# Hybrid layer on one core: the last q and k kept in SBUF, state-space gates fetched ahead and turned later, GLU banks swapped, residual loads on GpSimd's queue and later

## The chip, the cores and the metric

The kernel runs on one core of a Trainium2 chip. A core has five engines that run their own instruction streams in order and wait for each other on semaphores: PE (matmuls and transposes), DVE (elementwise), ACT (elementwise with functions), POOL (GpSimd; here it only issues DMAs) and SP (here it only issues DMAs). SBUF is the on-chip memory, PSUM holds what PE writes, HBM is the memory that DMAs reach. The metric is the time of one execution in microseconds (us); lower is better.

## The reference

One layer over 256 positions and 4096 channels, in float32:

```python
h = rmsnorm(x, ln_g)
p_x, p_gate, q, k, v, a_gate, s_u, s_gate = split(h @ w_in)     # 4096 -> 12288 columns
y_pool = pool_mixer(p_x, w_pool, pool_scale)                    # 1024 channels
y_attn = stick_breaking_attention(q, k, v)                      # 16 heads of 128
y_ssm  = s5_mixer(s_u, ...)       # scan, then GELU, then GLU: val * sigmoid(gate), 1024 channels
y = concat(rmsnorm(y_pool) * silu(p_gate), rmsnorm(y_attn) * silu(a_gate),
           rmsnorm(y_ssm) * silu(s_gate))
out = rmsnorm(x + y @ w_out, final_g)
```

In the attention, with z the scaled product of a query and a key, the weight is the exponential of log sigmoid(z) plus the sum, over the keys between, of log(1 - sigmoid(z)). The kernel forms that sum by matmuls with constant triangles (tneg, oneneg).

## The kernel before

**Units.** The work on PE is a row of units, each one block of output columns over all 4096 inputs: 16 narrow input units (512 columns: state-space input, pooling, gates, and v, q, k of the first attention groups), then the wide units w0 (v of groups 2 and 3) and w1 (q and k of group 3; 1024 columns each), then four narrow GLU units (glu0 to glu3, over 1024 inputs), w2 and w3 (gates of the attention), and out0 to out3 (the output projection). A wide unit has 32 sub-blocks of 12 matmuls; steps numbered in SEVEN take two sub-blocks as one seven-product (Strassen) form.

**Weights.** Each sub-block needs 512 KB of weights from HBM. SP's queue loads them into tiles w in the order of the program; LOAD_AHEAD gives four tiles ahead of PE, and two more are lent: tiles of tag u4 in w2 and w3, parts of the big output tile o in the out units. ACT copies a weight tile to its rounded part hi, DVE subtracts it to get lo, and three matmuls make one float32 product: lines 273 to 275 (hi and lo of weights against hi and lo of the rows, xhl, or hhl in the GLU), line 239 for the seven-product form, whose weight differences t DVE makes first.

**Side work.** Attention, state space and gates are written as generators, which `pump` advances between sub-blocks. A tile scheduler then orders the instructions of every engine but SP, whose order is the program's. Tiles come from pools by tag: k4 has six buffers, t4 three, u4 two. PSUM has four double banks in the wide stage: the running unit accumulates in two, and "side" work (products p7, transposes, ps_z, ps_av) uses the other two.

**Attention.** There are four groups of four heads, each in two pairs. For a pair PE makes ps_z from kt and qt and adds a mask (maskb); ACT and DVE make log terms al, split into ah and ax; PE adds the suffix sums of ah and then ax with tneg and oneneg (lines 704 to 706); ACT takes the exponential aw; PE multiplies by vt into ps_av; DVE copies to ao. v, q and k of group 2 and of group 3 go through HBM: `away` and `channels_away` write them (kept_v, kept_q, kept_k), `attention` fetches them, all on GpSimd's queue. Group 2's attention starts at the end of w0, group 3's at the end of w1, so that group 3 runs beside the GLU.

**State-space gates.** The output of the GLU (gl) is normalised by its sums, multiplied by a gate sgb, which GpSimd's queue fetches from HBM, and transposed (line 340) into the rows of the output projection.

**Out units.** At out0's sub-block 10 the big tile o is opened (`start_end`); its space is free after `place` has split the last rows into xhl on DVE (line 98). The residual x is loaded into o (line 892) on SP's queue, in order with the weights. `rows_again` fetches half of one block of rows again (yk, line 382).

Of the kernel before, what the change touches and what calls it, by code (L numbers as in the profile page):

```python
# [68 lines left out]
def body(tc, a, out, ctx):  # L69
# [84 lines left out]
    def load(i):  # L154
        ui, s, h = subs[i]
        kind, c, _ = units[ui]
        lent = i % (LOAD_AHEAD + 2) - LOAD_AHEAD
        if lent >= 0 and state["o"] is not None and kind == "out" and c < 3:
            w = state["o"][:, lent, 3 * WIDE:].rearrange("p (k n) -> p k n", k=2)
        elif lent >= 0 and hhl is not None and kind in WIDE_KINDS:  # L160
            w = mp.tile([P, 2, NU], F32, tag="u4", bufs=2, name="w")
        else:
            w = wp.tile([P, 2, NU], F32, tag="w", bufs=LOAD_AHEAD, name="w")
        nc.sync.dma_start(w, a["ws"][i])
        wtiles[i] = w
# [213 lines left out]

    def rows_again(s):  # L380
        t = bp.tile([P, 2, L], F32, tag="t4", bufs=T4, name="yk")
        nc.sync.dma_start(t, kept[s // 2][:, s % 2 * 2:s % 2 * 2 + 2, :])
        row_sums(s, t[:, 0, :], t[:, 1, :])
        row_difference(t[:, 0, :])
        hi_lo(xhl[:, 2 * s, 0, P:L], xhl[:, 2 * s, 1, P:L], t[:, 0, P:L])
# [277 lines left out]
    aout = {}  # L663
    att_sums = cp.tile([P, 2, 4], F32, name="att_sums")

    def attention(g, vt=None, qt=None, kt=None):
        if vt is None:
            vt, qt, kt = (mp.tile([P, 4, L], F32, tag="k4", bufs=K4, name=k + "t") for k in ("v", "q", "k"))
            for t, k in ((qt, "q"), (kt, "k"), (vt, "v")):
                G.dma_start(t, far[k, g])  # L670
            vt = vt.rearrange("p (t c) m -> p t (c m)", t=2)
            yield
        ao = mp.tile([P, 2, NU], F32, tag="k4", bufs=K4, name="ao")

        for pair in range(2):
            while state["po"] is not None and state["room"] < 7 and not state["draining"]:
                yield
            if state["po"] is None:
                z = pk.tile([P, 4, L], F32, tag="pz", bufs=1, name="ps_z")
            else:  # L680
                z = wide_bank(state["side"], "ps_z").rearrange("p h (c m) -> p (h c) m", c=2)
            state["held"] = True
            z0, z1 = z[:, 0:2, :], z[:, 2, :].rearrange("p (c m) -> p c m", c=2)
            for j in range(2):
                h = 2 * pair + j
                T.matmul(z0[:, j, :], kt[:, h, 0:P], qt[:, h, :], start=j == 0, stop=False, skip_group_check=True)  # L686
                T.matmul(z1[:, j, :], kt[:, h, P:L], qt[:, h, P:L], start=j == 0, stop=False, skip_group_check=True)
            mb = maskb.unsqueeze(1).broadcast_to([P, 2, P])
            T.matmul(z0[:, :, 0:P], identb, mb, start=False, stop=False, skip_group_check=True)
            T.matmul(z1, identb, mb, start=False, stop=False, skip_group_check=True)  # L690
            yield
            zz = z[:, 0:3, :]
            l = apool.tile([P, 3, L], F32, tag="al", bufs=1, name="al")
            log1pexp_parts(zz, l)
            yield
            stt(l, zz, 0.0, l, ALU.max, ALU.add)
            hi = apool.tile([P, 3, L], F32R, tag="ah", bufs=1, name="ah")
            lo = apool.tile([P, 3, L], F32R, tag="ax", bufs=1, name="ax")
            act(hi, l, AF.Copy)
            tt(lo, l, hi.bitcast(F32), ALU.subtract)  # L700
            yield
            for part in (hi, lo):
                l1 = part[:, 2, :].rearrange("p (c m) -> p c m", c=2)
                T.matmul(z0, tneg, part[:, 0:2, :], start=False, stop=False, skip_group_check=True)
                T.matmul(z0[:, :, P:L], oneneg, l1, start=False, stop=part is lo, skip_group_check=True)
                T.matmul(z1, tneg, l1, start=False, stop=part is lo, skip_group_check=True)
            yield
            w = apool.tile([P, 3, L], F32, tag="al", bufs=1, name="aw")
            act(w, zz, AF.Exp)
            yield  # L710
            if state["po"] is None:
                po = pk.tile([P, 2, 2, P], F32, tag="ps", bufs=2, name="ps_av")
            else:
                po = wide_bank(state["side"] + 1, "ps_av")[:, 0, :].rearrange("p (t c m) -> p t c m", t=2, c=2)
            for j in range(2):
                hs = slice((2 * pair + j) * P, (2 * pair + j) * P + P)
                w1 = w[:, 2, j * P:j * P + P]
                T.matmul(po[:, 0, j, :], w[:, j, 0:P], vt[:, 0, hs], start=j == 0, stop=True, skip_group_check=True)
                T.matmul(po[:, 1, j, :], w[:, j, P:L], vt[:, 0, hs], start=False, stop=False, skip_group_check=True)
                T.matmul(po[:, 1, j, :], w1, vt[:, 1, hs], start=False, stop=True, skip_group_check=True)  # L720
            yield
            V.tensor_copy(ao[:, :, pair * L:pair * L + L], po.rearrange("p t c m -> p t (c m)"))
            state["held"] = False
            yield
        square_sums(att_sums, ao, g)
        aout[g] = dp.tile([P, 2, NU], F32, name="kept_a%d" % g)
        G.dma_start(aout[g], ao)
        yield
# [160 lines left out]
    def load_rest(n):  # L889
        o = state["o"][:, :, n * WIDE:n * WIDE + WIDE]  # L890
        for h in range(2):
            nc.sync.dma_start(o[:, :, h * NU:h * NU + NU], a["xr"][2 * n + h])
        return o

    def load_fg(n):
# [4 lines left out]
    def finish(kind, c, n, ps):  # L900
# [34 lines left out]
        elif kind == "glu":  # L935
# [5 lines left out]
            if n % 2 == 0:  # L941
                def gate_gen(y=y):
                    sg = bp.tile([P, 2, NU], F32, tag="t4", bufs=T4, name="gs")
                    glu["sg"] = sg
                    sigmoid_of(y, sg)
                    yield
                side_q.append(gate_gen())
            else:
                def val_gen(y=y, n=n):
                    tt(y, y, glu.pop("sg"), ALU.mult)  # L950
                    yield
                    square_sums(glu_sums, y, n // 2)
                    yield
                    glu[n // 2] = y
                    if n == 3:
                        r = branch_norm(glu_sums, 1024)
                        for u in range(2):
                            yu = glu.pop(u)
                            sg = mp.tile([P, 2, NU], F32, tag="k4", bufs=K4, name="sgb")
                            G.dma_start(sg, sgate[u])  # L960
                            gated(yu, r, sg)
                            yield
                            yield from transposed(yu, keep(2 + u))
                side_q.append(val_gen())
        elif kind in WIDE_KINDS:
            e = state["joined"]
            parts = [(k, scaled_wide(ps, e, h, k + "z")) for h, (k, _) in enumerate(WIDE_IN[c])]
            for h, (k, z) in enumerate(parts):
                if k == "v":
                    away("v", 2 + h, z.rearrange("p t (c m) -> p (t c) m", m=L))  # L970
                elif k in ("q", "k"):
                    side_q.append(channels_away(k, 3, z))
                else:
                    gates.append(att_gate(2 * (c - 2) + h, z))
            if c < 2:
                side_q.append(attention(2 + c))
        elif kind == "out":
            o, e, fg = state["o_n"], state["joined"], state["fg"]
            for t in range(2):
# [10 lines left out]

    gates = []

    def gate_step(at):
        if at in (-1, 0):
            for g in gates:
                next(g)
        elif at in (5, 7):
            for _ in gates[0]:
# [6 lines left out]
    for i, (ui, s, h) in enumerate(subs):  # L1005
# [11 lines left out]
        if s == 0 and h == 0:  # L1017
# [12 lines left out]
            if wide:  # L1030
                ps = start_bank(kind, c)
            elif kind == "glu":
                state["side"] = 2
                pair = wide_bank(c % 2, "pm")
                ps = [pair[:, t, :] for t in range(2)]
            else:
                ps = [pm.tile([P, NU], F32, tag="c%d" % t, bufs=2, name="pm") for t in range(2)]
        if kind == "out" and (c > 0 and at == 0 or c == 0 and at == 10):
            if c == 0:
                start_end()  # L1040
            state["o_n"] = load_rest(c)
        while loaded < min(len(subs), i + 1 + LOAD_AHEAD + (2 if state["o"] is not None or kind in WIDE_KINDS and hhl is not None else 0)):
            if loaded == 0:
                load_first()
            else:
# [32 lines left out]
        if s == nk // 2 - 1 and h == (1 if wide else 0):  # L1078
            n = nth.get(kind, 0)
            nth[kind] = n + 1  # L1080
            if (kind, n) != ("out", 3):
                finish(kind, c if kind in WIDE_KINDS else n, n, ps)
            if gates:
                gate_step(-1)
        if kind == "out" and c == 0 and at == 11:
            rows_again(SEVEN[0])
# [5 lines left out]
                while state["held"]:  # L1092
                    pump(side_q, 1)
        elif wide and gates and at < 31:
            gate_step(at)
        elif wide and 1 <= at < 2 * SEVEN[0]:
            state["room"] = 2 * (2 * SEVEN[0] - at)
            pump(side_q, 2)
# [139 lines left out]
```

## Time and profile before

| | us |
|---|---|
| Three runs | 1558.12, 1563.12, 1563.67 |
| Median | 1563.12 |
| The profiled execution | 1561.29 |
| Its span in the trace | 1559.5 |
| PE busy | 1516.8 (97%) |
| DVE busy | 1268.5 (81%) |
| ACT busy | 899.0 (58%) |
| POOL busy | 16.4 (1%) |
| Mean granted clock of PE | 0.986 |

The span is what the trace covers; 1.8 us of the profiled execution lie around it. Times inside the program are counted from the span's start. The granted clock is the share of full speed that the chip's throttle gave PE. Busy time of an engine is time in which an instruction of it ran, at whatever clock.

### The profile page before, as it was taken

Reading aid. Unit: us, or ns where it says so; the run is one execution under the profiler, and the core shown is the slowest. Engines: PE = TensorE matmul, PEld = TensorE weight load, DVE = VectorE, ACT = ScalarE, POOL = GpSimd, SP = SyncE. Lnnn points to the kernel's source line nnn. Section 1 sums busy time; section 2 is a strip of 40 time slices with the busy share of each in tenths; the row PEclk is TensorE's granted clock in tenths of the full one; section 3 lists DMA queues with packets and bytes.
Section 4 is the critical chain, followed back from the end, with each engine's and each line's share of the span. In section 5 each row is a group of like instructions: output and inputs, shape, how many; then the busy total and the mean of one; then the engine's idle time right before and its main releaser. Section 6 shows DMA issues by size and latency. Waiting matters only on the chain.

```text
span 1559.5 us, 19518 instructions
## 1 busy us (share of the span) xinstructions
PE 1516.8 (97%) x6827; PEld 1232.6 (79%) x6827; DVE 1268.5 (81%) x1933; ACT 899.0 (58%) x1194; POOL 16.4 (1%) x34
## 2 busy tenths in 40 slices
PE   9999999999999999999999999879999799999996
PEld 7888788888787888788888888667888678888885
DVE  7479878898988978897788796558899698888886
ACT  7654546666555655465656556545767464645554
POOL 0000000000000000000000000000000000000000
PEclk9999999999999999999999999889999899999998
DMA  9866556666655656655757466637586476665654
GB/s 359 308 216 201 195 179 201 199 222 202 213 192 189 196 173 194 195 175 187 246 189 249 165 235 200 222 144 240 186 286 218 156 253 220 216 220 199 229 192 172
DMA packets 100978, 328.79 MB, mean 211 GB/s; under 512 B 12432, under 2 KB 18320, under 8 KB 100880
## 3 DMA queue, kind: packets, MB, share of 16 engines
q1 hardware_dynamic: 86416, 300.90, 56.9%
q0 software_dynamic: 4320, 15.73, 2.8%
q10 hardware_dynamic: 10144, 10.92, 2.4%
q8 instruction: 53, 0.87, 0.2%
q14 instruction: 45, 0.37, 0.1%
HBM read 310.73 MB, written 13.63 MB: 208 GB/s over the span
## 4 chain that ended last, share of the span: by engine, by line
PE 90%; DMA 3%; DVE 3%; ACT 2%; issue 1%; SPq 0%; DVEq 0%; ACTq 0%
PE pm L274 24%; PE pm L273 24%; PE pm L275 24%; PE p L239 7%; PE pm L239 5%; DMA w<-in_ws 3%; DVE lo L98 1%; DVE t L98 1%; PE ps_y L649 1%; ACT hi L110 1%; PE ps_z L686 1%; PE ps_c L778 1%; PE ps_bu L622 0%; PE ps_t L340 0%; PE ps_p L431 0%
## 5 line engine op out<-in xcount | busy, mean ns | idle before, releaser
L110 ACT ACTIVATE hi<-w 128x1024 fp32r<-128x1024 f32 (+1 forms) x505 | 509.8, 1017 | 423.3 <-PE pm L275 347.2
L98 DVE TENSOR_TENSOR lo<-w,hi 128x1024 fp32r<-128x1024 f32 (+1 forms) x505 | 587.0, 1170 | 184.6 <-ACT hi L110 182.0
L274 PE MATMUL pm<-lo,xhl 128*128 128x512 f32 x1672 | 655.4, 392 | 0.5 <-DVE lo L98 0.4
L275 PE MATMUL pm<-hi,xhl 128*128 128x512 f32 x1672 | 653.8, 391 | 0.0
L273 PE MATMUL pm<-hi,xhl 128*128 128x512 f32 x1672 | 646.6, 392 | 2.1 <-DVE ss_out L1123 0.8
L273 PEld LDWEIGHTS pm<-hi,xhl 128*128 128x128 f32 x1672 | 314.2, 188 | 72.4 <-issue 2.9
L274 PEld LDWEIGHTS pm<-lo,xhl 128*128 128x128 f32 x1672 | 314.2, 188 | 70.6 <-DVE lo L98 3.0
L275 PEld LDWEIGHTS pm<-hi,xhl 128*128 128x128 f32 x1672 | 314.2, 188 | 67.5 <-issue 2.1
L110 ACT ACTIVATE hi<-t 128x1024 fp32r<-128x1024 f32 x94 | 98.7, 1058 | 63.9 <-DVE t L98 31.8
L98 DVE TENSOR_TENSOR lo<-t,hi 128x1024 fp32r<-128x1024 f32 x94 | 113.2, 1220 | 8.7 <-ACT hi L110 8.2
L239 PE MATMUL p<-hi,xhl 128*128 128x512 f32 x188 | 74.4, 397 | 9.3 <-ACT hi L110 9.1
L239 PE MATMUL pm<-hi,xhl 128*128 128x512 f32 x188 | 75.6, 402 | 2.8 <-ACT hi L110 2.8
L98 DVE TENSOR_TENSOR t<-w 128x512 f32<-128x512 f32 x84 | 54.3, 687 | 29.1 <-DMA w<-in_ws 28.9
L239 PE MATMUL p<-hi,y 128*128 128x512 f32 x188 | 74.0, 394 | 0.1
L98 DVE TENSOR_TENSOR t<-w,t 128x512 f32<-128x512 f32 x84 | 57.5, 685 | 1.5 <-PE ps_t L340 1.2
L107 DVE SCALAR_TENSOR_TENSOR et<-et,pw,tr 128x16 f32<-128x16 f32 (+3 forms) x256 | 55.4, 275 | 2.0 <-ACT tr L110 1.6
L110 ACT ACTIVATE tr<-et,pw 128x32 f32<-128x32 f32 (+3 forms) x128 | 44.2, 382 | 11.1 <-DVE et L107 6.8
L239 PEld LDWEIGHTS p<-hi,xhl 128*128 128x128 f32 x188 | 35.5, 189 | 18.2 <-ACT hi L110 9.6
L239 PEld LDWEIGHTS pm<-hi,xhl 128*128 128x128 f32 x188 | 35.9, 191 | 11.9 <-ACT hi L110 4.1
L239 PEld LDWEIGHTS p<-hi,y 128*128 128x128 f32 x188 | 35.3, 188 | 8.9 <-ACT hi L110 1.0
L637 DVE TENSOR_TENSOR_SCAN tb<-rho,ta 128x256 f32<-128x256 f32 x64 | 40.5, 674 | 0.3
L110 ACT ACTIVATE hi<-o 128x1024 fp32r<-128x1024 f32 (+1 forms) x26 | 25.0, 976 | 24.6 <-PE pm L275 23.6
(266 smaller groups left out, 1286.8 us busy)
## 6 DMA issues: line engine op xcount, KB each, us to landing
w<-in_ws SPq DMA_DIRECT2D x501, 512.0 KB, 4.2
o<-in_ws SPq DMA_DIRECT2D x26, 512.0 KB, 4.3
xsq<-in_xr SPq DMA_DIRECT2D x8, 512.0 KB, 6.7
o<-in_xr SPq DMA_DIRECT2D x8, 512.0 KB, 7.0
xt<-in_xT SPq DMA_DIRECT2D x15, 256.0 KB, 6.1
b<-in_bst ACTq DMA_DIRECT2D x16, 192.0 KB, 4.6
u<-uT ACTq DMA_DIRECT2D x96, 32.0 KB, 2.8
kept<-yT POOLq DMA_DIRECT2D x6, 512.0 KB, 5.6
```

Source lines behind the costliest of these rows:

```text
L98: V.tensor_tensor(o, x, y, op)
L107: V.scalar_tensor_tensor(o, x, s, y, op0, op1)
L110: return S.activation(o, x, f, **kw)
L239: T.matmul(o, stat[:, p, :], pair[q][:, n], start=start and k == 0, stop=stop and k == 2, skip_group_check=True)
L273: T.matmul(ps[t], stat[:, slot, 0, sl], hi[:, n], start=begin, stop=False, skip_group_check=True)
L274: T.matmul(ps[t], stat[:, slot, 0, sl], lo[:, n], start=False, stop=False, skip_group_check=True)
L275: T.matmul(ps[t], stat[:, slot, 1, sl], hi[:, n], start=False, stop=end, skip_group_check=True)
L637: V.tensor_tensor_scan(tb[:, c, :], rho[:, pr:pr + 1].broadcast_to([P, L]), ta[:, c, :], 0.0, ALU.mult, ALU.add)
L649: T.matmul(ps[32 * j:32 * j + 32, 0:L], cf[:, j, c, :], ss[j][:, c, :], start=c == 0, stop=c == 1, skip_group_check=True)
L686: T.matmul(z0[:, j, :], kt[:, h, 0:P], qt[:, h, :], start=j == 0, stop=False, skip_group_check=True)
L778: T.transpose(ps[:, (c * 2 + t) * P:(c * 2 + t + 1) * P], z[:, t, (h * 2 + c) * P:(h * 2 + c + 1) * P], ident)
```

## The change

It has five parts.

1. Attention takes vt, qt and kt from its caller. A function `fetch` loads group 2's v, q and k in one go at the end of w0. Of group 3 only v is fetched, at the end of w1; its q and k are transposed into two SBUF tiles of tag u4 and stay there, ahead of the rest of the side queue. The lent weight tiles of tag u4 are therefore left to w3's sub-blocks alone: w2 has four weight tiles.
2. The state-space gates sgb are fetched when glu3 is written, the product goes into them, and their transposes become steps of w2, at its sub-blocks 5 and 7.
3. The GLU accumulates in banks 2 and 3, its side work uses 0 and 1; before, the other way round.
4. The residual loads and the fetch in `rows_again` go from SP's queue to GpSimd's.
5. The tile o is opened, and its first residual load issued, at out0's sub-block 14 instead of 10.

```diff
@@ load()
-        elif lent >= 0 and hhl is not None and kind in WIDE_KINDS:
+        elif lent >= 0 and kind == "w3":
             w = mp.tile([P, 2, NU], F32, tag="u4", bufs=2, name="w")
@@ rows_again()
-        nc.sync.dma_start(t, kept[s // 2][:, s % 2 * 2:s % 2 * 2 + 2, :])
+        G.dma_start(t, kept[s // 2][:, s % 2 * 2:s % 2 * 2 + 2, :])
@@
-    def attention(g, vt=None, qt=None, kt=None):
-        if vt is None:
-            vt, qt, kt = (mp.tile([P, 4, L], F32, tag="k4", bufs=K4, name=k + "t") for k in ("v", "q", "k"))
-            for t, k in ((qt, "q"), (kt, "k"), (vt, "v")):
-                G.dma_start(t, far[k, g])
-            vt = vt.rearrange("p (t c) m -> p t (c m)", t=2)
-            yield
+    def fetch(g, kinds):
+        got = []
+        for k in kinds:
+            t = mp.tile([P, 4, L], F32, tag="k4", bufs=K4, name=k + "t")
+            G.dma_start(t, far[k, g])
+            got.append(t.rearrange("p (t c) m -> p t (c m)", t=2) if k == "v" else t)
+        return got
+
+    def attention(g, vt, qt, kt):
@@ load_rest()
-            nc.sync.dma_start(o[:, :, h * NU:h * NU + NU], a["xr"][2 * n + h])
+            G.dma_start(o[:, :, h * NU:h * NU + NU], a["xr"][2 * n + h])
@@ finish(), kind "glu"
                         for u in range(2):
-                            yu = glu.pop(u)
-                            sg = mp.tile([P, 2, NU], F32, tag="k4", bufs=K4, name="sgb")
-                            G.dma_start(sg, sgate[u])
-                            gated(yu, r, sg)
-                            yield
-                            yield from transposed(yu, keep(2 + u))
+                            yu, sg = glu.pop(u), sgs[u]
+                            for t in range(2):
+                                stt(sg[:, t, :], yu[:, t, :], r[:, t:t + 1], sg[:, t, :], ALU.mult, ALU.mult)
+                            gates.append(transposed(sg, keep(2 + u)))
+                        yield
+                sgs = []
+                if n == 3:
+                    for u in range(2):
+                        sgs.append(mp.tile([P, 2, NU], F32, tag="k4", bufs=K4, name="sgb"))
+                        G.dma_start(sgs[u], sgate[u])
@@ finish(), wide kinds
-                    side_q.append(channels_away(k, 3, z))
+                    t = mp.tile([P, 4, L], F32, tag="u4", bufs=2, name=k + "t")
+                    side_q.insert(h, channels(z, t, QS if k == "q" else 1.0))
+                    cur[k] = t
...
-            if c < 2:
-                side_q.append(attention(2 + c))
+            if c == 0:
+                side_q.append(attention(2, *fetch(2, "vqk")))
+            elif c == 1:
+                side_q.append(attention(3, *fetch(3, "v"), cur["q"], cur["k"]))
@@ gate_step()
-            for g in gates:
+            for g in gates if kind != "w2" else ():
@@ the loop over sub-blocks
-                state["side"] = 2
-                pair = wide_bank(c % 2, "pm")
+                state["side"] = 0
+                pair = wide_bank(2 + c % 2, "pm")
...
-        if kind == "out" and (c > 0 and at == 0 or c == 0 and at == 10):
+        if kind == "out" and (c > 0 and at == 0 or c == 0 and at == 14):
...
-        while loaded < min(len(subs), i + 1 + LOAD_AHEAD + (2 if state["o"] is not None or kind in WIDE_KINDS and hhl is not None else 0)):
+        while loaded < min(len(subs), i + 1 + LOAD_AHEAD + (2 if state["o"] is not None or kind == "w3" else 0)):
...
-            if gates:
+            if gates and wide:
                 gate_step(-1)
...
-            gate_step(at)
+            gate_step(at, kind)
```

Three places in the order of the instructions. The first is PE in the second pair of attention group 2, from its mask matmul on (names carry buffer numbers). Before, the GLU's matmuls (pm from hhl) stand behind it:

```order
L690 MATMUL ps_z_8508<-maskb_84,identb_83 128x256
L273 MATMUL pm_8489<-hi_8436,hhl_8484 128x512
L274 MATMUL pm_8489<-lo_8437,hhl_8484 128x512
L275 MATMUL pm_8489<-hi_8436,hhl_8484 128x512
L273 MATMUL pm_8489<-hi_8436,hhl_8484 128x512
```

After, the same mask matmul stands in w1 (line numbers are two higher):

```order
L692 MATMUL ps_z_7909<-maskb_84,identb_83 128x256
L239 MATMUL pm_7784<-hi_8102,y7_6899 128x512
L239 MATMUL pm_7784<-lo_8103,y7_6899 128x512
L239 MATMUL pm_7784<-hi_8102,y7_6899 128x512
L706 MATMUL ps_z_7909<-ah_7939,tneg_81 128x512
L707 MATMUL ps_z_7909<-ah_7939,oneneg_82 128x2x128
L708 MATMUL ps_z_7909<-ah_7939,tneg_81 128x256
L706 MATMUL ps_z_7909<-ax_7940,tneg_81 128x512
L707 MATMUL ps_z_7909<-ax_7940,oneneg_82 128x2x128
L708 MATMUL ps_z_7909<-ax_7940,tneg_81 128x256
L720 MATMUL ps_av_8001<-vt_7778,aw_7985 128x128
```

The pair moved from the GLU into w1, and instead of 43 matmuls three (one product of w1's last seven-product step) stand between its mask and its suffix sums.

The second is PE at the transposes of the state-space gates (ps_t from ident). Before, they follow the last ps_av of group 3 and six matmuls of w2 (pm from xhl):

```order
L720 MATMUL ps_av_8812<-vt_8653,aw_8792 128x128
L273 MATMUL pm_9019<-hi_9214,xhl_102 128x512
L274 MATMUL pm_9019<-lo_9215,xhl_102 128x512
L275 MATMUL pm_9019<-hi_9214,xhl_102 128x512
L273 MATMUL pm_9019<-hi_9214,xhl_102 128x512
L274 MATMUL pm_9019<-lo_9215,xhl_102 128x512
L275 MATMUL pm_9019<-hi_9214,xhl_102 128x512
L340 MATMUL ps_t_8980<-ident_80,gl_8747 128x128
L340 MATMUL ps_t_8987<-ident_80,gl_8747 128x128
```

After, they stand in the sub-blocks of w2:

```order
L275 MATMUL pm_8982<-hi_9057,xhl_102 128x512
L273 MATMUL pm_8982<-hi_9057,xhl_102 128x512
L340 MATMUL ps_t_9091<-ident_80,sgb_8952 128x128
L340 MATMUL ps_t_9098<-ident_80,sgb_8952 128x128
L274 MATMUL pm_8982<-lo_9058,xhl_102 128x512
```

They moved from six matmuls behind group 3's last ps_av to 82 behind it.

The third is SP at out0, where yk at line 367 is the last block of rows that w3 fetches. Before:

```order
L367 DMA yk<-kept_109 128x1024
L164 DMA w<-in_ws 128x1024 x15
L892 DMA o<-in_xr 128x2x512 x2
L164 DMA w<-in_ws 128x1024 x4
L382 DMA yk<-kept_106 128x512
L164 DMA o<-in_ws 128x1024 x2
```

After:

```order
L367 DMA yk<-kept_109 128x1024
L164 DMA w<-in_ws 128x1024 x19
L164 DMA o<-in_ws 128x1024 x2
L164 DMA w<-in_ws 128x1024 x4
L164 DMA o<-in_ws 128x1024 x2
```

The residual and yk left SP's queue; the 15 and the 4 weights now follow each other, and the first two lent tiles (o from in_ws) come next.

More of the change, by code (lines that the diff above doesn't have):

```diff
@@ L991, in body, with gate_step @@
     gates = []
-    def gate_step(at):
+    def gate_step(at, kind=None):
         if at in (-1, 0):
-            for g in gates:
+            for g in gates if kind != "w2" else ():
                 next(g)
```

## The prediction, made before the changed kernel ran

> **What bounds the kernel now.** I read the page's engine table and slices first, then the windows table where the slices dip, then PE's timeline inside the dips, then what each first instruction behind a dip had waited for.
>
> ```profile
> PE 1516.8 (97%) x6827; PEld 1232.6 (79%) x6827; DVE 1268.5 (81%) x1933; ACT 899.0 (58%) x1194; POOL 16.4 (1%) x34
> PEclk9999999999999999999999999889999899999998
> ```
>
> PE is busy for 97% of the span, and the granted clock falls in three slices (25, 26 and 31, of 39 us each) besides the last. The windows table (PE's busy time is its second number, the granted clock the third from the right) says how much lies there:
>
> ```profile
> 987.30:997.60 10.30, 6.09 (x18) 4.98 (x19) 0.00 (x0) 1.65 (x2) 0.00 (x0) 0.50 0.69 279
> 1035.10:1048.80 13.70, 6.96 (x19) 4.98 (x20) 10.21 (x22) 5.92 (x15) 0.54 (x1) 0.50 0.57 187
> 1236.50:1246.80 10.30, 4.04 (x9) 2.75 (x10) 4.10 (x6) 4.22 (x5) 0.00 (x0) 0.50 0.96 371
> 840.00:980.00 140.00, 140.00 (x641) 115.36 (x640) 107.99 (x118) 83.58 (x97) 3.75 (x7) 1.00 0.65 217
> 1280.00:1520.00 240.00, 240.00 (x1047) 195.99 (x1046) 207.77 (x225) 130.28 (x141) 0.00 (x0) 1.00 0.63 217
> ```
>
> In the last two rows PE is never idle. Outside the holes there is nothing to gain but matmuls, and the change takes none away. PE's timeline (in brackets: idle time before, and what ended it) names the holes:
>
> ```profile
> 991.51 0.76 PE L686 MATMUL ps_z<-qt,kt 128*128 128x256 f32 x1 [6.39 <-issue]
> 1039.08 2.11 PE L340 MATMUL ps_t<-ident,gl 128*128 128x128 f32 x8 [6.23 <-DVE gl L107]
> 1043.79 0.79 PE L239 MATMUL pm<-hi,xhl 128*128 128x512 f32 x1 [2.60 <-ACT hi L110]
> 1242.72 0.79 PE L239 MATMUL p<-hi,xhl 128*128 128x512 f32 x1 [9.14 <-ACT hi L110]
> ```
>
> A hole costs its idle time and, at clock 0.50, half of the busy time in the half-clock window. Hole 1 (start of the GLU): 6.39 + 6.09/2 = 9.4 us. Hole 2 (start of w2): 6.23 + 2.60 + 6.96/2 = 12.3. Hole 3 (out0): 9.14 + 4.04/2 = 11.2. Together 32.9 us.
>
> **The change, part by part.**
>
> *Last q and k in SBUF.* Hole 1 is attention group 3 waiting for kt, written to HBM and fetched again on GpSimd's queue:
>
> ```profile
> 982.41 0.54 POOL L670 DMA_DIRECT2D kt<-kept_k  x1 [9.04 <-DMA w<-in_ws]
> DMA to landing us min/median/max: 9.0/9.1/9.3
> ```
>
> 982.41 + 9.0 is 991.4, where PE resumes. Without that trip nothing holds the product, which now comes after q and k are transposed on chip. -9.4; the four DMAs of q and k of group 3 and their 2 x 0.54 us of issues go with it.
>
> *Group 2 moves.* It is fetched in one go at w0's end, and both its head pairs now stand in w1. Here is the price. First, the fetch: vt is issued at
>
> ```profile
> 858.79 0.55 POOL L670 DMA_DIRECT2D vt<-kept_v x1 [3.71 <-DMA kept_v<-vz]
> DMA to landing us min/median/max: 6.7/8.8/10.9
> ```
>
> so kt follows at 858.79 + 2 x 0.55 = 859.9 and lands between 866.6 and 870.8. Its first product moves 48 matmuls later than now (861.0, below), at 0.228 us each (six in 1.37, at hole 3), to about 871.9: no wait, with 1 us to spare at worst. Second, the second pair. Before, 43 matmuls of the GLU stood between its mask matmul and the suffix sums (tneg, oneneg); now three do, and PE takes its instructions in order. What PE must then sit through is seen at the pair whose chain stands in w1 before (tile ps_z, and ACT's and DVE's timelines):
>
> ```profile
> L686 PE MATMUL ps_z<-qt,kt x4: 377/378/382, 861.0 to 861.9; 128*128 128x256 f32 x4
> ...
> L690 PE MATMUL ps_z<-maskb,identb x1: 273/273/273, 862.4 to 862.4; 128*128 128x256 bf16 x1
> 864.35 0.61 ACT L110 ACTIVATE hi<-w 128x512 fp32r<-128x512 f32 x1
> 866.95 1.06 ACT L110 ACTIVATE hi<-t 128x1024 fp32r<-128x1024 f32 x1 [1.25 <-PE pm L275]
> 867.91 0.83 ACT L110 ACTIVATE ah<-al 128x768 fp32r<-128x768 f32 x1
> 869.18 0.95 DVE L98 TENSOR_TENSOR ax<-al,ah 128x768 fp32r<-128x768 f32 x1
> L706 PE MATMUL ps_z<-ax,tneg x1: 282/282/282, 874.7 to 874.7; 128*128 128x256 f32 x1
> 875.03 0.81 ACT L110 ACTIVATE aw<-ps_z 128x768 f32<-128x768 f32 x1 [1.47 <-PE ps_z L706]
> ```
>
> From the mask matmul at 862.4 to the end of ah at 868.74 are 6.3 us, with two weight copies of ACT inside, 0.61 and 1.06. In the new order one stands between: 5.7. PE has its own mask matmul and three others, 0.9, so it idles 4.8. Then ax is done 0.95 + 0.1 after ah, while ah's three matmuls take 0.7: idle 0.3. Then aw comes 0.3 after the last tneg and takes 0.81: idle 0.9 before the products with vt. 6.0 us idle. The clock fell 2.2, 2.3 and 2.9 us into the three gaps (start less idle gives 985.1, 1032.8 and 1233.6; the half-clock rows begin at 987.3, 1035.1 and 1236.5) and stayed down 10.3 us or more, so it falls here too: 10.3 less the 3.5 us still idle leaves 6.8 busy, half of it lost, 3.4. +9.4, between 6 (two copies fewer, no drop) and 11 (both copies inside).
>
> [...]
>
> *SSM gates earlier and turned later.* Hole 2's transposes wait for this chain (DVE's timeline):
>
> ```profile
> 1036.73 0.16 DVE L395 TENSOR_REDUCE s_b<-glu_sums 128x2 f32<-128x4 f32 x1 [4.56 <-ACT junk L110]
> 1038.18 1.41 DVE L107 SCALAR_TENSOR_TENSOR gl<-gl,r_b,sgb 128x512 f32<-128x512 f32 x2
> ```
>
> Behind the wait of 4.56 (for ACT's squares of the last attention output) it runs alone on DVE until 1039. In the new order the products into sg stand on DVE among w2's splits, and the transposes 82 matmuls into w2, 82 x 0.228 = 18.7 us. What stands ahead on DVE there:
>
> ```profile
> L98 DVE TENSOR_TENSOR lo<-w,hi 128x1024 fp32r<-128x1024 f32 (+1 forms) x505 | 587.0, 1170 | 184.6 <-ACT hi L110 182.0
> L98 DVE TENSOR_TENSOR t<-w 128x512 f32<-128x512 f32 x84 | 54.3, 687 | 29.1 <-DMA w<-in_ws 28.9
> w<-in_ws SPq DMA_DIRECT2D x501, 512.0 KB, 4.2
> ```
>
> After the output copy come the splits of w2's sub-blocks 6 and 7 (some 3.2 us into w2), then two differences (t, 2 x 0.69) of sub-block 9, and only then the split of sub-block 4. w2 now has four weight tiles ahead, not six (the two of tag u4 hold q and k), so sub-block 9 is loaded once 7 is split: it lands 4.2 to 6.6 us later (6.6: the weight row at hole 3, below), and the split of 4 ends at 3.2 + 4.2 + 1.4 + 1.2 = 10.0 to 12.4. PE wants it 50 matmuls in, at 11.4. I take a stall of 1.0 (0 to 3). Three more splits and the norm's small steps bring the products to about 15 to 16, ahead of 18.7: hidden, with 3 us to spare. At the GLU's end, group 3's last aw (0.3 + 0.81) stands uncovered: 1.2. -12.3 + 2.2.
>
> *GLU banks swapped.* No instruction is added. The GLU now starts in the banks of w1's side work, which are read out long before w1 ends, and the third pair waits for q and k in any case: nothing (0 to 1).
>
> *Residual loads.* Hole 3 is a queue: SP stood at the first residual load, with weights behind it.
>
> ```profile
> SPq L892 <- DVE xhl L98: 21.8, 1, 21.8
> 1233.59 1.31 SPq L892 DMA_DIRECT2D o<-in_xr x2
> 1234.94 6.64 DMA w<-in_ws
> 1241.61 1.06 ACT L110 ACTIVATE hi<-w 128x1024 fp32r<-128x1024 f32 x1 [9.31 <-DMA w<-in_ws]
> 1229.80 0.48 PE L239 MATMUL pm<-hi,xhl 128*128 128x512 f32 x1
> 1227.80 1.37 PE pm L239 x6
> ```
>
> The residual goes to GpSimd's queue, where only write-backs and yk are ahead of it and out0 needs it only at its join, after its last seven-product pair: nothing. On SP the four weights go first, but then come two weight tiles lent from the same big tile, which is free no sooner: 1233.59. A lent tile then lands at 1233.6 + 6.6 = 1240.2 and is split by 1241.3. PE's last matmul ahead of it is the 44th after the transposes, 1229.80 + 44 x 0.228 = 1239.8. Stall 1.5 us, from 0 (the median landing of weights, 4.2) to 6 (9.1, as for kt). -11.2 + 1.5.
>
> Sum: -32.9 + 9.4 + 2.2 + 1.5 = -19.8. The profiled execution took 1561.29 us, so 1541.5; it lies 1.8 below the median, 1563.12, of runs from 1558.12 to 1563.67. I take 1541.
>
> **The rivals.**
>
> B, the pair in w1 costs less: ACT's copy falls elsewhere, PE finds its way through in under 4 us and the clock stays up. For it: the trace shows no gap of 3 to 6 us, so no price for one. Against it: all three drops came before 3 us. Time 1541.5 - 3.4 - 1.2 = 1537. [...]
>
> C, hole 3 stays: lent tiles wait behind the same release, and each landing over 6.6 us, likely while the residual comes down at once (DMA share was 0.96 there), stalls PE by 6 to 9 us with the half clock. 1541.5 - 1.5 + 9.5 = 1549.5.
>
> D, slower: four tiles ahead starve w2. Each of its six seven-product pairs would lose a landing and a clock drop, 4.2 + 3 = 7.2, 43 in all: 1585. It decides when a weight lands later than three sub-blocks of 12 matmuls, 3 x 2.7 = 8.2 us, after its slot is freed. Against it: w1 runs on four tiles too, and 840 to 980 is 140.00 of 140 busy.
>
> E, the holes refill: what waited for kt waits instead for q's transposes, w2 for its gates, out0 for lent tiles, within 0.5% of before. Against it: each new waiter was given 44 matmuls or more of cover in the order, but for w1.
>
> **How the numbers follow.** Forecast 0.57 (1536 to 1547, by the ends of its terms), B 0.13, C 0.15, E 0.08, D 0.07. The range must reach from B's lower end (1537 with no stall at the GLU's end, w2 and out0 is 1533, less half the runs' spread of 5.6: 1530) to C's upper one (1549.5 and w2's worst, 1554); it leaves out D and E. Faster by over 0.5% (7.8 us, about what a measurement of this kernel tells from none): A, B and C, 0.85; E 0.08; slower 0.07.
>
> **What would show it.** PE at full clock from 980 to 1030 in the old count; a new gap of 4 to 6 us in w1, ended by ACT's ah, and a half clock behind it; no gap ahead of the SSM transposes; SP's 21.8 us wait gone or moved to the lent tile, and at most 2 us of PE's idle there. I am wrong if w2 shows gaps at its seven-product pairs, if w1's gap is longer than 7 us, or if PE's rate falls outside the gaps.

## The result and the profile after

The changed kernel took 1541.26 us (median of four runs, 1539.24 to 1546.88) where the kernel before took 1563.22 in the same session: ratio 0.9873, 95% interval 0.9840 to 0.9905. Run again beside the later experiments it took 1539.59 (0.9868, 0.9854 to 0.9881). The profiled execution took 1541.22 us, its span is 1539.4 against 1559.5 before.

The page of the changed kernel, PE's line and the granted clock, shows the three slices at 8 gone:

```profile
PE 1512.4 (98%) x6827; PEld 1229.3 (80%) x6827; DVE 1266.5 (82%) x1933; ACT 896.0 (58%) x1194; POOL 20.5 (1%) x39
PEclk9999999999999999999999999999999999999998
```

PE's timeline of the changed kernel. These are the gaps that are left between 840 and 1240 above 0.6 us:

```profile
895.32 0.79 PE L706 MATMUL ps_z<-ah,tneg 128*128 128x512 f32 x1 [4.68 <-ACT ah L110]
898.43 0.79 PE L720 MATMUL ps_av<-vt,aw 128*128 128x128 f32 x2 [0.90 <-ACT aw L110]
1008.18 0.49 PE L720 MATMUL ps_av<-vt,aw 128*128 128x128 f32 x2 [0.91 <-ACT aw L110]
1037.03 0.50 PE L274 MATMUL pm<-lo,xhl 128*128 128x512 f32 x1 [0.96 <-DVE lo L98]
```

Holes 1, 2 and 3 have no successor at their places. The one new gap of over 1 us, 4.68 us, is in w1 and waits for ah, as forecast. The windows table gives the half clock behind it, and PE's work at out:

```profile
895.35:902.17 6.82, 5.92 (x21) 5.17 (x22) 1.60 (x2) 0.86 (x2) 0.00 (x0) 0.50 0.00 0
1280.00:1500.00 220.00, 220.00 (x960) 179.68 (x959) 188.63 (x205) 120.65 (x130) 1.42 (x2) 1.00 0.60 201
```

The new gap costs 4.68 + 0.90 + 5.92/2 = 8.5 us. How it comes about stands on ACT's and DVE's timelines of the changed kernel:

```profile
890.03 0.81 ACT L110 ACTIVATE al<-ps_z 128x768 f32<-128x768 f32 x1 [2.93 <-PE ps_z L692]
890.74 1.05 ACT L110 ACTIVATE hi<-t 128x1024 fp32r<-128x1024 f32 x1
891.69 1.71 ACT L110 ACTIVATE al<-al 128x768 f32<-128x768 f32 x2
893.43 0.96 DVE L107 SCALAR_TENSOR_TENSOR al<-ps_z,al 128x768 f32<-128x768 f32 x1 [0.38 <-ACT al L110]
894.42 0.84 ACT L110 ACTIVATE ah<-al 128x768 fp32r<-128x768 f32 x1 [1.03 <-DVE al L107]
```

One copy of weights (hi from t) stands inside the chain. From the start of al to the end of ah are 5.2 us, and PE has three matmuls to do meanwhile.

### The profile page after: what moved, and what is told of

Same layout as the page of the kernel before. It is cut to its first block, busy times and chain, and to the rows that moved or that the text cites. A ratio compares the mean times of both kernels' runs of the same rounds, so it can differ in the third digit from the quotient of the medians.

```text
span 1539.4 us, 19528 instructions
## 1 busy us (share of the span) xinstructions
PE 1512.4 (98%) x6827; PEld 1229.3 (80%) x6827; DVE 1266.5 (82%) x1933; ACT 896.0 (58%) x1194; POOL 20.5 (1%) x39
## 4 chain that ended last, share of the span: by engine, by line
PE 85%; DVE 6%; DMA 5%; ACT 2%; issue 2%; SPq 0%; DVEq 0%; ACTq 0%
PE pm L274 23%; PE pm L275 23%; PE pm L273 23%; PE p L239 7%; PE pm L239 5%; DMA w<-in_ws 5%; DVE lo L98 3%; DVE t L98 1%; ACT hi L110 1%; PE ps_y L649 1%; PE ps_c L780 1%; PE ps_bu L622 1%; PE ps_z L688 0%; PE ps_p L431 0%; PE ps_t L340 0%
```

## The experiments

Eleven variants ran, and the changed kernel again. All edits are on the kernel before (B) or the changed kernel (A). The table gives PE's idle gaps in us at each place in the profiled execution of each kernel: all of 0.6 us or more in these places, and some smaller ones; 0 means none above 0.25. Half clocks are not included. The last column is the ratio to runs of the kernel before on the same chip; for the variants and the second run of the changed kernel their medians were 1560.0, 1560.3 and 1560.7.

| kernel | w1 | GLU start | GLU end, w2 | out0 | us | ratio, 95% |
|---|---|---|---|---|---|---|
| before | 0 | 6.39 | 6.23 + 2.60, 0.87 | 9.14 | 1563.22 | 1 |
| changed | 4.68 + 0.90 | 0 | 0.91 + 0.96 | 0 | 1541.26 | 0.9873 (0.9840 to 0.9905) |
| qk_only | 4.67 + 0.90 | 0 | 0 | 8.94 + 1.16 | 1549.86 | 0.9935 (0.9915 to 0.9955) |
| ssm_only | 0 | 4.61 | 6.19 | 9.21 | 1557.93 | 0.9985 (0.9975 to 0.9996) |
| w2_four_tiles | 0 | 2.50 | 7.64 + 2.60 | 8.95 | 1560.94 | 0.9998 (0.9986 to 1.0010) |
| residual_undone | 4.68 + 0.90 | 0 | 0.91 + 0.91 | 5.48 | 1550.64 | 0.9941 (0.9923 to 0.9959) |
| queue_only | 0 | 3.12 | 6.23 + 2.60, 0.88 | 2.30 | 1550.84 | 0.9945 (0.9924 to 0.9965) |
| later_only | 0 | 5.39 | 6.24 + 2.60, 0.88 | 0.63 + 0.53 | 1551.96 | 0.9948 (0.9934 to 0.9961) |
| banks_back | 4.68 + 0.90 | 0 | 0 | 1.71 | 1539.74 | 0.9868 (0.9850 to 0.9885) |
| pair2_back | 0.45 | 0 | 0.96, 6.24 + 0.90 | 0.45 | 1540.54 | 0.9877 (0.9858 to 0.9896) |
| qk_early | 0.64 | 0 | 0.91 + 0.99 | 0.28 | 1534.30 | 0.9836 (0.9816 to 0.9856) |
| early_banks_back | 0.65 | 0 | 0 | 0 | 1528.04 | 0.9800 (0.9786 to 0.9814) |
| early_plain | 0.66 | 0 | 0 | 0 | 1527.34 | 0.9788 (0.9774 to 0.9801) |
| changed, again | 4.68 + 0.90 | 0 | 0.91 + 0.48 | 0 | 1539.59 | 0.9868 (0.9854 to 0.9881) |

### Is w1's gap a matter of cover? pair2_back and qk_early

```diff
 A, pair2_back
     def attention(g, vt, qt, kt):
+        if g == 2:
+            yield
```

> The changed kernel with one step of delay ahead of attention group 2, so that its second pair goes back from w1 into the GLU. Theory (what costs is the lack of cover, wherever it is): w1's gap (4.68 + 0.90 us idle and about 2.7 of half clock) is gone, but now group 3's last pair at the GLU's end has no weight matmuls at all between its mask and its suffix sums, so a gap of 5 to 6 us with a half clock stands there: 1540 to 1543. Rival (the GLU has room for three pairs, the price was w1's): w1's 8 us are saved, 1533.

The theory held. PE's timeline of pair2_back at the GLU's end:

```profile
1003.61 0.79 PE L708 MATMUL ps_z<-ah,tneg 128*128 128x512 f32 x1 [6.24 <-ACT ah L110]
1006.73 0.79 PE L722 MATMUL ps_av<-vt,aw 128*128 128x128 f32 x2 [0.90 <-ACT aw L110]
```

The gap has left w1 and stands where group 3's last pair now has no matmul of its own to hide behind. The time cannot be told from the changed kernel's. In both kernels one pair is left without enough matmuls to cover its chain.

```diff
 A, qk_early
+        if kind == "w0" and at == 20:
+            state["qk2"] = fetch(2, "qk")
...
-                side_q.append(attention(2, *fetch(2, "vqk")))
+                side_q.append(attention(2, *fetch(2, "v"), *state["qk2"]))
```

> The changed kernel with group 2's q and k fetched in w0 (at its sub-block 20), v as before. Their first product then needs no landing at w1's start, both pairs start earlier, and 41 matmuls instead of 3 stand between the second pair's mask and its suffix sums. Theory (w1's gap is missing cover on PE, begun by the late landing of kt): idle in w1 below 1 us, no half clock, 1541.3 - 8 = 1533. Rival (ACT and DVE are too full in w1 for two pairs): the chain grows with the cover, the gap stays, 1539 to 1542.

The theory held: w1 is left with one gap of 0.64 us, the granted clock was 1.00 from 840 to 980 and from 1000 to 1260, and the time is 1534.30. PE's timeline of qk_early, the first product of the group and that gap:

```profile
858.47 0.59 PE L688 MATMUL ps_z<-qt,kt 128*128 128x256 f32 x2
897.39 0.50 PE L239 MATMUL p<-hi,y 128*128 128x512 f32 x1 [0.64 <-ACT hi L110]
```

ACT and DVE had room enough for two pairs. What used up the start of w1 was the landing of kt. In the changed kernel (POOL's timeline, the tile's landing time, PE's timeline) it was

```profile
861.78 0.53 POOL L670 DMA_DIRECT2D kt<-kept_k  x1
DMA to landing us min/median/max: 8.0/8.0/8.0
873.22 0.59 PE L688 MATMUL ps_z<-qt,kt 128*128 128x256 f32 x2
```

PE did not wait there: the product stands behind enough matmuls that it need not. Fetched in w0, it starts 14.7 us earlier, and the matmuls that then stand behind it cover the second pair.

### Which part closed hole 2? qk_only and ssm_only

qk_only is B with the attention part and w2's four tiles, ssm_only is B with the state-space gate part. Both take the hunks shown above, of which the core is

```diff
 B, qk_only (part 1)
-            if c < 2:
-                side_q.append(attention(2 + c))
+            if c == 0:
+                side_q.append(attention(2, *fetch(2, "vqk")))
+            elif c == 1:
+                side_q.append(attention(3, *fetch(3, "v"), cur["q"], cur["k"]))
 B, ssm_only (part 2)
-                            gated(yu, r, sg)
-                            yield
-                            yield from transposed(yu, keep(2 + u))
+                            gates.append(transposed(sg, keep(2 + u)))
```

> The kernel before with the attention part alone (group 2 fetched in one go, group 3's q and k in SBUF, w2 on four weight tiles); gates, banks and residual as before. Numbers relative to the kernel before. In its order the old transposes of the state-space gates stand 63 matmuls (14 us) behind group 3's last product instead of 6. Theory 1 (each part closes its own hole): hole 1 is closed (-9.4), w1's gap appears (+8.7), holes 2 and 3 stay: -1 to +2 us. Theory 2 (group 3 done earlier is what closes hole 2 as well, since its transposes waited for the squares of that attention's output): also -9 to -12: 1548 to 1552 where before is 1560.

> The kernel before with the state-space gate part alone (fetched at glu3, product into the gate's tile, transposes at w2's sub-blocks 5 and 7). Theory 1 (each part closes its own hole): hole 2's 12.3 us shrink to 3, holes 1 and 3 stay: -9 us, about 1551 where before is 1560. Theory 2 (the cover came from group 3 being done earlier): its last pair still ends late, the transposes still stand 6 matmuls behind its last product, hole 2 stays within 4 us: 1556 to 1560.

Theory 2 held in both, and the prediction had put the gain down to the other part. PE's, ACT's and DVE's timelines of ssm_only:

```profile
1031.01 0.63 ACT L110 ACTIVATE junk<-ao 128x512 bf16<-128x512 f32 x1 [3.79 <-DVE ao L722]
1035.54 0.16 DVE L395 TENSOR_REDUCE s_b<-glu_sums 128x2 f32<-128x4 f32 x1 [4.55 <-ACT junk L110]
1036.99 2.74 DVE L107 SCALAR_TENSOR_TENSOR sgb<-gl,r_b,sgb 128x512 f32<-128x512 f32 x4
1037.84 2.16 PE L340 MATMUL ps_t<-ident,sgb 128*128 128x128 f32 x8 [6.19 <-issue]
```

ACT takes its instructions in order, and in that order the squares of the last attention output (ao) come ahead of those of gl. So the gates' norm waits for group 3's last pair (4.55 us, second row), whichever way the gates are then turned, and in ssm_only that pair still ends at 1030, with the transposes 6 matmuls behind it. Of hole 2 only the 2.60 us gap went. In qk_only the gates are as before, and hole 2 is gone (DVE's and PE's timelines):

```profile
1025.36 0.75 DVE L107 SCALAR_TENSOR_TENSOR gl<-gl,r_b,sgb 128x512 f32<-128x512 f32 x1
1030.86 0.38 PE L340 MATMUL ps_t<-ident,gl 128*128 128x128 f32 x2
```

Group 3's last product starts at 1016.2 there. The chain from it to the first gated gl is no shorter, 9.9 us against 7.8 before, but 63 matmuls of w2 lie over it.

### Four tiles in w2: w2_four_tiles

```diff
 B
-        elif lent >= 0 and hhl is not None and kind in WIDE_KINDS:
+        elif lent >= 0 and kind == "w3":
...
-... kind in WIDE_KINDS and hhl is not None else 0)):
+... kind == "w3" else 0)):
```

> The kernel before with four weight tiles in w2 instead of six and nothing else. Theory (four tiles feed w2 as they feed w1, a late split at its start costs 0 to 3 us): 1560 to 1563 where before is 1560. Rival D (w2's seven-product pairs starve, each with a gap): 1580 or more.

No difference that can be measured. Rival D falls: beyond hole 2 no gap of over 0.25 us stands in w2. Hole 2's own place can hide a small cost here: its first gap was 7.64 us instead of 6.23.

### The residual: residual_undone, queue_only, later_only

```diff
 B, queue_only (part 4; residual_undone takes it back from A, and part 5 with it)
-            nc.sync.dma_start(o[:, :, h * NU:h * NU + NU], a["xr"][2 * n + h])
+            G.dma_start(o[:, :, h * NU:h * NU + NU], a["xr"][2 * n + h])
 B, later_only (part 5)
-        if kind == "out" and (c > 0 and at == 0 or c == 0 and at == 10):
+        if kind == "out" and (c > 0 and at == 0 or c == 0 and at == 14):
```

> The changed kernel with the residual loads and the half block of rows back on SP's queue and the output tile opened at sub-block 10. Theory (hole 3 was SP's queue blocked by the residual): the 9 us gap and its half clock are back, 1541.3 + 11.2 = 1552. Rival (the gap came from w3 running late after the other holes, or the lent tiles wait just as long): within 3 us of 1541.

> The kernel before with the residual loads and the half block of rows on GpSimd's queue, the output tile still opened at sub-block 10. Theory (the place in SP's queue counts, not the sub-block): SP issues 19 weights before a lent tile, hole 3 is gone, 1563.2 - 11.2 = 1552, hole 1 and hole 2 as before. Rival (opening later is what counts, since the lent tiles wait for the same release): hole 3 stays, 1560 to 1563.

> The kernel before with the residual loads still on SP, but the output tile opened and the first of them issued at out0's sub-block 14. SP then issues 19 weights ahead of it and the two lent tiles behind it. Theory (what counts is how many weights SP issues ahead of the first load that waits for the output tile, not whose queue the residual is in): hole 3 shrinks to 2 to 4 us, 1550 to 1552 where before is 1560, like queue_only. Rival (the residual on SP is the trouble wherever it stands): hole 3 stays, 1558 to 1560.

PE's timeline of residual_undone, with SP's waits, then of queue_only and of later_only:

```profile
1232.82 0.80 PE L239 MATMUL p<-hi,xhl 128*128 128x512 f32 x1 [5.48 <-ACT hi L110]
SPq L894 <- DVE xhl L98: 18.0, 1, 18.0
```

```profile
1249.55 0.50 PE L239 MATMUL p<-hi,y 128*128 128x512 f32 x1 [2.30 <-ACT hi L110]
```

```profile
1244.36 0.50 PE L239 MATMUL p<-hi,xhl 128*128 128x512 f32 x1 [0.63 <-ACT hi L110]
```

Undone, the hole is back: 0.9941 against 0.9868 to 0.9873, so the two parts are worth some 11 us of 1560; the interval of each ratio reaches 2 to 5 us to either side. Its idle time was 5.5 us, not 9.1, so the expectation's reason was right and its size of the idle time was not; that the time came out as expected is partly luck. Either half alone closes most of the hole: in queue_only and in later_only SP issues 19 weights instead of 15 ahead of the first load that waits for the output tile, and waits 11.8 us for the tile's release instead of 21.8. Moving the load and delaying it both do that. Whether the two halves together are worth more than one (8 to 9 us each on B) cannot be told within the intervals.

### The GLU's banks, and the best version

```diff
 A, banks_back
-                state["side"] = 0
-                pair = wide_bank(2 + c % 2, "pm")
+                state["side"] = 2
+                pair = wide_bank(c % 2, "pm")
```

early_banks_back has this edit and qk_early's on A. early_plain is qk_early's edit and parts 1, 4 and 5 on B: the gates and the banks are those of before.

> The changed kernel with the GLU accumulating in banks 0 and 1 again and its side work in 2 and 3. As predicted the swap is worth 0 to 1 us either way. In its order group 3's last pair runs on into w2 (its side banks are w2's too), with 7 and 25 of w2's matmuls between its steps, while in the changed kernel it must end before w2 opens banks 0 and 1. Theory (the swap costs the 0.9 us gap before ps_av at the GLU's end and gives nothing): 1540. Rival (the swap lets the GLU start before w1's results are read out of banks 0 and 1): a gap of 2 to 4 us at the GLU's start, 1543 to 1546.

> The changed kernel with q and k of group 2 fetched in w0 and the GLU's banks as before the change. Theory: w1's gap (4.7 + 0.9 and the half clock) and the GLU's end (0.9) are both closed, the gains add: 1540 - 8 - 1 = 1531. Rival (in run banks_back the 0.9 was regained at out0, 1.7 us there): 1533 to 1534, as qk_early.

> The kernel before with the attention part, q and k of group 2 fetched in w0, and the residual part; state-space gates and GLU banks as before the change. Theory (hole 2 was closed by group 3 ending earlier, so the gate part adds nothing): 1531 to 1533, as early_banks_back. Rival (the gate part is worth some us once the rest is in): 1534 to 1540.

> The changed kernel once more, beside the versions below. It should keep the ratio 0.987 (about 1540 where before is 1560), with w1's gap of 4.7 us in the profile; its half clock may last two or three of the 3.4 us steps seen so far, by where the gap falls among them.

banks_back closed the 0.91 us at the GLU's end: with the old banks group 3's last pair may run on into w2, whose side banks are the same two, while the swap makes it end before w2 opens banks 0 and 1. No gap came at the GLU's start. Over the whole kernel the difference to the changed kernel cannot be told from none. It is not zero on the way: w3's last transposes (ps_t from ya) start at 1217.7 in banks_back, at 1222.3 and 1220.4 in the two profiles of the changed kernel, and the gap of 1.71 us at out0 gives part of that lead back. Beside qk_early's edit, where out0 has no such gap, the old banks were worth more than expected: 0.9800 against 0.9836, 5.6 us of 1560. Of the 5.8 us between those two profiled spans, 1.2 come before the GLU, where the code of the two is the same (qk_early has a gap of 1.68 us at 834), and 4.6 from the GLU on. Of these, 0.91 and 0.99 are gaps at the GLU's end and in w2; the cause of the rest stays open.

early_plain equals early_banks_back, so part 2 adds nothing that can be measured once group 3 ends earlier. It is the best version, 1527.34 us, 12 us below the changed kernel on the same chip. Its page and a window over the middle of the span:

```profile
PE 1508.0 (99%) x6827; PEld 1227.0 (80%) x6827; DVE 1267.7 (83%) x1933; ACT 897.1 (59%) x1194; POOL 20.5 (1%) x39
PEclk9999999999999999999999999999999999999998
840.00:1500.00 660.00, 658.75 (x2932) 536.65 (x2931) 560.65 (x645) 402.60 (x469) 14.77 (x25) 1.00 0.64 220
```

PE is idle for 1.25 us of 660 and never at half clock there. What bounds this stretch now is PE's own matmuls.

## Why the prediction was right, point by point

**Time.** 1541 was forecast, 1541.26 came. That they agree within 1 us is partly luck. With the sizes that the runs showed (holes of 32.9 us gone, 8.5 new in w1, 0.91 + 0.96 left at the GLU's end and in w2, nothing at out0) the sum is -22.5, where the profiled span lost 20.0. The missing 2.5 us are smaller gaps of PE (1.2 us more idle time than before) and 1.3 us more busy time outside the half clock; their cause was not traced.

**Hole 1** went, as forecast. Its size was not a constant: the same wait took 2.50 to 6.39 us in the five profiles that have it. The prediction took the largest, from the one profile that it had.

**w1's price.** Forecast 9.4 us, measured 8.5: idle 4.8 + 0.3 + 0.9 against 4.68 + 0 + 0.90, and half clock 3.4 against 2.96. The chain from rows of the earlier pair, with one copy instead of two, was read rightly. The first product came at 873.2, forecast 871.9, with no wait for kt, as forecast. That the clock would fall was right; it fell 4.7 us after the gap's start, where the prediction had 2.2 to 2.9 (last section).

**Hole 2.** The term's size was right (-12.3 + 2.2, measured 0.91 + 0.96 left), but it stood in the wrong line. The step that failed is the one headed "SSM gates earlier and turned later": it credited that part with what part 1 does. The prediction quoted the row that says so, the 4.56 us wait for ACT's squares "of the last attention output", and did not draw from it that the end of group 3 sets the norm. Measured, ssm_only gained 2 us (0.6 to 3.9), qk_only 10, with hole 2 shut.

The products into sg were forecast for 15 to 16 us into w2 and the transposes for 18.7. DVE's and PE's timelines of the changed kernel, where group 3's last product starts at 1009.4:

```profile
1023.40 2.73 DVE L107 SCALAR_TENSOR_TENSOR sgb<-gl,r_b,sgb 128x512 f32<-128x512 f32 x4
1028.30 0.38 PE L340 MATMUL ps_t<-ident,sgb 128*128 128x128 f32 x2
1034.55 1.29 DVE L98 TENSOR_TENSOR t<-w 128x512 f32<-128x512 f32 x2 [3.48 <-DMA w<-in_ws]
```

Done at 1026.1, used at 1028.3. The stall for weights was forecast at 1.0 for the split of sub-block 4, 11 us into w2. None came there. One of 0.96 came 28 us in, behind a difference t that waits for a weight (third row), and was 0.48 in the second run: that the size agrees is luck.

**GLU banks**, forecast at nothing: the 1.2 us at the GLU's end that the prediction charged to group 3's last pair (0.91 measured) go with the swap, as banks_back has no gap there. Over the whole changed kernel the swap's cost cannot be told from none, as forecast; beside qk_early's edit it was 5.6 us.

**Hole 3.** Forecast 1.5 us left, measured none. SP's timeline and waits, and POOL's, of the changed kernel:

```profile
1222.79 0.80 SPq L164 DMA_DIRECT2D o<-in_ws  x2
SPq L164 <- DVE xhl L98: 4.8, 1, 4.8
1223.31 4.26 POOL L894 DMA_DIRECT2D o<-in_xr  x6 [24.11 <-DVE lo L98]
```

The lent tiles do wait for the same release, 4.8 us of SP's time instead of 21.8, and the residual follows them on POOL's queue. Rival C, that this wait would reopen the hole, fell in this run. In banks_back and queue_only, where SP waited 11.8 us for that release, gaps of 1.71 and 2.30 us stand at out0, so it was close.

**Rivals.** B fell (4.68 us instead of under 4, and the clock did drop, to 0.50 for 6.82 us), D fell in w2_four_tiles and in the profile after, E fell.

## What to carry to other kernels

Price a moved chain by the matmuls that stand over it in the new order, not by the place it leaves: PE in order pays the whole chain where its cover is missing, and moving the chain only moves the bill, as pair2_back did (4.68 us in w1 became 6.24 at the GLU's end). When several engines' chains meet in one wait, follow the in-order queue of the engine named (here ACT's squares of ao ahead of those of gl) before crediting an edit with the gain. A late load that makes nobody wait may still cost, because the instructions that need it stand later in the order; fetching group 2's q and k 12 sub-blocks earlier was worth some 5 us, while the best version does without parts 2 and 3.

## What the runs showed of the hardware

In the kernel before, the clock was at 0.50 for 10.24, 13.66 and 10.24 us (from 987.32, 1035.10 and 1236.49), in the changed kernel for 6.82 us (from 895.35), before the half clock at the end of the program: 3, 4, 3 and 2 times 3.41 us. These are windows of that length at the gaps (PE's busy time is the second number), first three of the kernel before and two of the changed kernel, then one of its second run and one of queue_only:

```profile
983.91:987.32 3.41, 1.20 (x6) 0.65 (x4) 2.61 (x3) 2.15 (x3) 0.10 (x1) 1.00 0.94 347
1031.69:1035.10 3.41, 1.16 (x5) 0.58 (x4) 0.48 (x1) 2.80 (x8) 1.06 (x2) 1.00 0.39 154
1233.08:1236.49 3.41, 0.49 (x3) 0.06 (x1) 0.48 (x1) 0.00 (x0) 0.00 (x0) 1.00 0.41 121
```

```profile
888.53:891.94 3.41, 2.10 (x13) 1.53 (x11) 0.73 (x2) 1.91 (x3) 0.00 (x0) 1.00 0.00 0
891.94:895.35 3.41, 0.03 (x1) 0.04 (x1) 2.12 (x3) 2.27 (x3) 0.00 (x0) 1.00 0.00 0
```

```profile
888.72:892.13 3.41, 1.14 (x8) 0.64 (x6) 1.09 (x1) 2.84 (x4) 0.00 (x0) 1.00 0.00 0
```

```profile
1245.40:1248.81 3.41, 1.85 (x9) 1.16 (x7) 1.92 (x3) 1.31 (x2) 0.00 (x0) 1.00 1.03 399
```

At the end of the first three, the fifth and the sixth the clock fell; in these PE was busy for 35, 34, 14, 1 and 33%. At the end of the fourth (62% busy) and the last (54%) it did not. The prediction was wrong to take a fixed delay of 2.2 to 2.9 us from three cases: in the changed kernel the fall came 4.7 us after the gap's start, in its second run 2.3, for the same gap of 4.68 us. What sets the moment is not shown by these cases. The mean granted clock of the two profiled executions was 0.995 and 0.993, with the same gaps of 4.68 and 0.90 us in w1; that the same gap can cost a half clock of different length may be one source of the spread between runs of one kernel, the author's estimate, which was not tried by itself.
